# A layer's input projection by Strassen-Winograd products: when the saved partial products are read back

## The chip, the cores and the metric

One core of a Trainium2 chip runs the kernel; the seven other cores are idle. The metric is device time of one execution in microseconds. Three runs of the kernel before gave 1662.98, 1666.43 and 1667.63 us, so the median is 1666.43 us. The profile shows one further execution, which took 1667.98 us.

## The reference

One layer of a streaming encoder with 1024 tokens and width 2048, all in float32. One projection of the input gives ten blocks of columns; a sparse attention group (each query keeps its 256 best keys by a light indexer) and a Mamba-2 state-space group (causal convolution, chunked scan, gated RMS norm) work on them; both are gated, joined, projected back, added to the scaled input and normalised:

```python
u = jnp.einsum('bsd,de->bse', h, w_in[layer])
q, k, v, z_attn, q_idx, k_idx, w_idx, z_ssd, xbc, dt_raw = _split_cols(u, IN_WIDTHS)
o_attn = _dsa_attention(q, k, v, q_idx, k_idx, w_idx) * jax.nn.silu(z_attn)
o_ssd = _ssd_mixer(xbc, z_ssd, dt_raw, conv_w[layer], ...)
mixed = jnp.concatenate([o_attn, o_ssd.astype(o_attn.dtype)], axis=-1)
sub = jnp.einsum('bse,ed->bsd', mixed, w_out[layer])
h = _layer_norm(DEEPNORM_ALPHA * h + sub, ln_g[layer], ln_b[layer])
```

The change concerns the first line, the input projection.

## The kernel before, in words

**Number format.** Every float32 operand of the two projections is split into a high and a low part: ACT rounds the high part (`xh` of the input, `wh` of the weights), DVE subtracts it to get the low part (`xl`, `wl`). A product is three matmuls: `wh` with `xh`, `wh` with `xl`, `wl` with `xh`.

**Units.** The input projection is cut into 190 units, numbered 0 to 189 here in the order in which PE runs them (the list `pieces` of `units()`). A unit is a 128-column block of weights times half the input's depth: eight blocks of depth by three matmuls of 128x512, that is 24 matmuls into one PSUM bank (`pj`). Four banks have that name. The output projection follows as units 190 to 245. Between the matmuls of a unit the program places PE work of the other parts: indexer scores, attention, state-space scan.

**Seven products for eight.** Most weight blocks are handled in pairs by a Strassen-Winograd scheme (`product()`), seven units for what eight would do, in four phases. There are two groups of pairs: group 0 with 8 pairs, group 1 with 14. In a phase the pairs go in couples: first half-unit of both, then second half-unit of both. Phase 0's first unit is saved to DRAM as P1 (`t_save`, copied out of PSUM by ACT). Phase 1 adds P1 to its two units and saves the sums as U2 and U3 (`t_u`, on DVE). Phases 2 and 3 add U2 or U3 to what PE has computed (`t_comb`, on DVE) and hand the result on. In phases 0 to 2 the second unit of a pair accumulates on top of the first one's PSUM bank, so PE may not begin it before ACT or DVE has read the bank (the event `after`); that unit comes two units after the first.

**The loads concerned.** A saved partial product comes back by one 256 KB load from DRAM into a buffer of tag `u` (128x512 float32). There are 29 such buffers, used by nearly everything in the kernel. `pre_ld()` makes a task of it, and `t_ld()` asks for a free buffer with two more to spare (`u=1, keep=2`) and for the saved data to be there; then it puts the load on SP's queue. There are 88 of these loads. The DVE addition that uses one is placed after the last matmul of the unit.

**What sets the order.** Every engine runs its instructions in the order in which the program was written, and that order is written by a planner in the kernel (`Flow`): it keeps a list of tasks by priority, and at four points of each unit (`pump`) lets every task that is ready by its own cost table write its next instructions. `hooks` are calls at the start of a unit: requests for partial products, requests for the next set of inputs, and so on. The table of costs only decides the order; on the chip, each instruction waits for what it needs and blocks the later ones of its engine. Weights are loaded up to eight units ahead, and the split into `wh` and `wl` is written up to two units ahead where data and buffers allow (`w_split`, `need_w`).

In the profile every instruction has line L312, since one helper writes them all; groups are told apart by the names of tiles. `u<-pj,u` and `cv<-pj,u` on DVE are the additions of a partial product; `u<-u` on SP's queue is a load of U2 or U3 or a save of one (110 in all), `u<-p` a load of P1 (22), `p<-u` a save of P1.

Of the kernel before, what the change touches and what calls it, by code (L numbers as in the profile page):

```python
# [582 lines left out]
class Layer:  # L583
# [20 lines left out]
    def units(self):  # L604

        pieces, work = [], []
        self.hooks = {}
        self.sets = []
        self.mate = {}

        def put(p, listed=True):
            if listed:
                work.append((len(pieces), None))
            pieces.append(p)
            return len(pieces) - 1

        def plain(h, tile, u, n):
            kind, j = tile
            t = ORDER.index(tile)
            p = Piece("T", h, t, u, load=(("w", t, u),), n=n + u, open=u == 0, close=u == 1, key=(h, t),  # L620
                      s0=256 if (kind == "qi" and h == 0) else 0)
            if u == 1:
                p.done = lambda ps: self.fl.add(getattr(self, "t_" + kind)(h, j, ps), 0, f"{kind}{j}h{h}", self.fl.t + 100)
            put(p)

        for pairs in PLAN:
            if isinstance(pairs, tuple):
                h, tiles, end = pairs
                n = len(self.sets)
                self.sets += [("x", h, 0), ("x", h, 1)]  # L630
                for part in [tiles[:3]] + [[t] for t in tiles[3:-end]] + [tiles[-end:]]:
                    for u in range(2):
                        for tile in part:
                            plain(h, tile, u, n)
                continue
            gi = GROUPS.index(pairs)
            if self.sets[-2:] != [("x", 0, 0), ("x", 0, 1)]:
                self.sets += [("x", 0, 0), ("x", 0, 1)]
            base = len(self.sets) - 2
            self.sets += [("f", "M2"), ("f", "M3"), ("f", "S1"), ("f", "S4"), ("x", 1, 1)]  # L640
            couples = [list(range(c, min(c + 2, len(pairs)))) for c in range(0, len(pairs), 2)]
            if len(couples[-1]) == 1:
                couples[-2:] = [couples[-2] + couples[-1]]
            for ph in range(4):
                if (gi, ph) in ((0, 2), (1, 0)):
                    self.hooks.setdefault(len(pieces), []).append(lambda on=gi == 0 and ph == 2: setattr(self.fl, "resting", on))
                for couple in [int(k) if k.isdigit() else k for k in OPENING] if (gi, ph) == (0, 0) else couples:
                    if isinstance(couple, str):
                        tile = ("misc", 0) if couple == "m" else QI["abcdefgh".index(couple)]
                        for u in range(2):  # L650
                            plain(0, tile, u, base)
                        continue
                    couple = couples[couple] if isinstance(couple, int) else couple
                    for f in range(1 + (ph < 3)):
                        for c in couple:
                            i = put(self.product(gi, c, pairs[c], ph, f, base + 2 * ph + f))
                            if f:
                                self.mate[gi, c, ph] = i
                            if ph and (ph, f) != (1, 1):
                                self.hooks.setdefault(max(i - 1, 0), []).append(lambda gi=gi, c=c, ph=ph, f=f: self.pre_ld(gi, c, ph, f))  # L660
        end = {}
        for i, p in enumerate(pieces):
            end[p.n] = i
        for i in end.values():
            pieces[i].last = True
        freed = sorted(end, key=end.get)
        for n in range(2, len(self.sets)):
            at = end[freed[n - 2]] - 2
            self.hooks.setdefault(at, []).append(lambda n=n: self.request(n))
        self.n_t = len(pieces)  # L670
        self.hooks.setdefault(self.n_t - 6, []).append(lambda: self.forms(0))
        self.hooks.setdefault(12, []).append(self.form_tasks)
        for half in range(2):
            self.hooks.setdefault(12, []).append(lambda half=half: self.fl.add(self.t_wsum(half), 5, "wsum"))
        for n in range(7):
            for d in range(2):
                for j in range(4):
                    if n < 6 or 4 * d + j < 8 - SKEW:
                        work.append((len(pieces), (0, 1, 2, 3)))
                    name = PRODUCTS[n][1]  # L680
                    pieces.append(Piece("O", n, d, j, load=(("o", name, d, j),)))
        for sts in ((0,), (1,), (2,), (3,)):
            work += [(len(pieces) - SKEW + j, sts) for j in range(SKEW)]
        return pieces, work
# [1672 lines left out]
```

## Time and profile before

| What | Value |
|---|---|
| Median of three runs | 1666.43 us (1662.98 to 1667.63) |
| The profiled execution: time, and span of its instructions | 1667.98 us, 1666.1 us |
| PE busy, share of the span | 1620.1 us, 97% |
| DVE busy | 1321.7 us, 79% |
| ACT busy | 1002.0 us, 60% |
| POOL busy | 197.3 us, 12% |
| DMA packets | 414.48 MB, mean 249 GB/s |
| Mean granted TensorE clock | 0.992 |

A wait in brackets in the order of time is the idle time of the engine just before the instruction, with what ended it. In the table of waits each row gives who waited for whom, microseconds in total, how often, and the longest. The 1.9 us between the profiled execution's time and its span lie outside of the instructions. The second group of the input projection runs from about 570 to 1313 us, the output projection from there to 1654 us, and the last 11 us have no matmul.

### The profile page before, as it was taken

To read this page: it belongs to the slowest core of one execution; us is meant where nothing else is said; L and a number is where in the kernel's file an instruction comes from. 1 tells how busy PE (TensorE), PEld (TensorE's weight loads), DVE (VectorE), ACT (ScalarE), POOL (GpSimd) and SP (SyncE) were. 2 spreads that over 40 slices of the span, in tenths; PEclk is the share of its full clock that TensorE was granted. 3 is DMA by queue.
4 is the path that set the end of the run, shared out by engine and by line. 5 is a ranking of instruction groups with operands and counts; after the bars stand their busy time and mean duration, and the time that the engine had idled before them with its cause. 6 is when DMAs were issued, how large, how long until landed. Compare 5 with 4: busy or idle time off the path is not lost. (4 is left out here: it accounts for less than half of the span.)

```text
span 1666.1 us, 23979 instructions
## 1 busy us (share of the span) xinstructions
PE 1620.1 (97%) x7996; PEld 1340.9 (80%) x7996; DVE 1321.7 (79%) x2429; ACT 1002.0 (60%) x1770; POOL 197.3 (12%) x215
## 2 busy tenths in 40 slices
PE   9999999999998989999999999999999999999997
PEld 7787777888787768888888888888877888888885
DVE  5889998997778866788676669875787687659998
ACT  4555666779787788776344456776866555532330
POOL 0100010000000000122212202222010000100110
PEclk9999999999999999999999999999999999999999
DMA  8177574789768856687786584656988889668664
GB/s 309 52 280 258 189 262 168 268 303 334 290 230 324 294 196 234 235 304 277 260 288 218 180 286 161 210 171 210 334 284 307 316 300 325 215 232 274 220 202 152
DMA packets 192387, 414.48 MB, mean 249 GB/s; under 512 B 19720, under 2 KB 55688, under 8 KB 192264
## 3 DMA queue, kind: packets, MB, share of 16 engines
q1 hardware_dynamic: 191832, 412.56, 71.7%
q8 instruction: 63, 1.03, 0.2%
q14 instruction: 60, 0.49, 0.1%
q10 hardware_dynamic: 432, 0.39, 0.1%
HBM read 308.94 MB, written 103.94 MB: 248 GB/s over the span
## 5 line engine op out<-in xcount | busy, mean ns | idle before, releaser
L312 PE MATMUL pj<-xh,wh 128*128 128x512 f32 (+1 forms) x1496 | 585.7, 392 | 14.5 <-ACT u L312 6.0
L312 PE MATMUL pj<-xh,wl 128*128 128x512 f32 (+1 forms) x1496 | 573.6, 383 | 5.1 <-DVE wl L312 5.1
L312 PE MATMUL pj<-xl,wh 128*128 128x512 f32 (+1 forms) x1496 | 573.0, 383 | 0.0
L312 DVE TENSOR_TENSOR wl<-wr,wh 128x1024 fp32r<-128x1024 f32 (+2 forms) x236 | 282.4, 1201 | 172.4 <-ACT wh L312 170.4
L312 PEld LDWEIGHTS pj<-xh,wh 128*128 128x128 f32 x1496 | 283.8, 190 | 68.6 <-issue 7.5
L312 PEld LDWEIGHTS pj<-xh,wl 128*128 128x128 f32 x1496 | 283.5, 190 | 63.1 <-DVE wl L312 7.3
L312 PEld LDWEIGHTS pj<-xl,wh 128*128 128x128 f32 x1496 | 284.0, 190 | 49.1
L312 ACT ACTIVATE wh<-wr 128x1024 fp32r<-128x1024 f32 (+2 forms) x242 | 248.1, 1031 | 120.0 <-PE pj L312 82.8
L312 PE MATMUL a<-u,u 128*128 128x512 f32 (+3 forms) x736 | 172.8, 354 | 7.6 <-DVE s L312 4.4
L312 PEld LDWEIGHTS a<-u,u 128*128 128x128 f32 x736 | 120.7, 189 | 42.5 <-DVE s L312 18.6
L312 ACT ACTIVATE u<-a 128x512 fp32r<-128x512 f32 (+4 forms) x115 | 53.2, 479 | 153.3 <-DVE u L312 58.0
L312 ACT ACTIVATE u<-s,sm 128x640 bf16<-128x640 int16 (+7 forms) x132 | 129.7, 983 | 22.1 <-DVE sm L312 20.0
L312 DVE TENSOR_TENSOR u<-u,u 128x512 f32<-128x512 f32 (+6 forms) x204 | 128.6, 645 | 5.7 <-DMA u<-wo 1.3
L312 PE MATMUL pj<-wh,xh 128*128 128x512 f32 x310 | 125.2, 404 | 0.5 <-DVE u L312 0.5
L312 PE MATMUL pj<-wh,xl 128*128 128x512 f32 x310 | 121.0, 390 | 0.0
L312 PE MATMUL pj<-wl,xh 128*128 128x512 f32 x310 | 121.0, 390 | 0.0
L312 ACT ACTIVATE a<-a 128x512 f32<-128x512 f32 (+3 forms) x160 | 77.1, 505 | 68.3 <-PE a L312 65.5
L312 ACT ACTIVATE u<-u 128x512 f32<-128x512 f32 (+4 forms) x146 | 80.1, 558 | 52.4 <-DVE u L312 43.9
L312 DVE TENSOR_TENSOR u<-pj,u 128x512 f32<-128x512 f32 (+2 forms) x112 | 74.7, 668 | 45.7 <-PE pj L312 42.2
L312 DVE TENSOR_TENSOR wr<-wr,wr 128x1024 f32<-128x1024 f32 (+1 forms) x81 | 99.8, 1233 | 0.8 <-DMA wr<-wt 0.4
L312 POOL TENSOR_SCALAR s<-s,sm 128x640 f32<-128x640 f32 (+7 forms) x64 | 63.8, 1011 | 124.0 <-DVE sm L312 97.4
L312 DVE SCALAR_TENSOR_TENSOR u<-cv,cw,u 128x512 f32<-128x512 f32 x96 | 73.0, 766 | 6.7 <-ACT u L312 3.5
(259 smaller groups left out, 2200.3 us busy)
## 6 DMA issues: line engine op xcount, KB each, us to landing
wr<-wt SPq DMA_DIRECT2D x187, 512.0 KB
u<-u SPq DMA_DIRECT2D x110, 256.0 KB
wr<-t SPq DMA_DIRECT2D x44, 512.0 KB
u<-wo SPq DMA_DIRECT2D x64, 256.0 KB
ts<-u SPq DMA_DIRECT2D x64, 256.0 KB
wr<-ts SPq DMA_DIRECT2D x32, 512.0 KB
s<-xt SPq DMA_DIRECT2D x24, 512.0 KB
t<-wr SPq DMA_DIRECT2D x22, 512.0 KB
```

The source lines that it names most:

```text
L312: f(*args, **kw)
```

## The change

The request for a partial product is hooked at the start of the unit two before the one that it is added to, where it was one before. Buffers, priorities and costs stay.

```diff
@@ units() @@
                             if ph and (ph, f) != (1, 1):
-                                self.hooks.setdefault(max(i - 1, 0), []).append(lambda gi=gi, c=c, ph=ph, f=f: self.pre_ld(gi, c, ph, f))
+                                self.hooks.setdefault(max(i - 2, 0), []).append(lambda gi=gi, c=c, ph=ph, f=f: self.pre_ld(gi, c, ph, f))
```

Of the 88 loads, 85 stand earlier against PE's units, nearly all by one unit. Since the planner then finds other buffers free at each point, the order of everything after the first such load changes with it. Rows of the two orders follow; numbers at the end of a name tell buffers apart and differ between the programs.

SP's queue where the first loads stand, during units 50 to 53, before. `p1_0_0` and `p1_0_1` are P1 of pairs 0 and 1, `xf...` and `wt` are inputs and weights, `c0_0` takes a result:

```order
L312 DMA p1_0_7_3490<-u_629_3476 128x512
L312 DMA xr_632_3498<-xfM32_107 128x1024
L312 DMA s4_633_3506<-xfM33_108 128x1024
L312 DMA wr_638_3530<-wt 128x1024
L312 DMA wr_639_3531<-wt 128x1024
L312 DMA wr_640_3532<-wt 128x1024
L312 DMA u_646_3553<-p1_0_0_1661 128x512
L312 DMA c0_0_333<-u_635_3518 128x512
L312 DMA u_666_3626<-p1_0_1_1741 128x512
```

The same place with the change:

```order
L312 DMA p1_0_7_3490<-u_629_3476 128x512
L312 DMA u_632_3492<-p1_0_0_1661 128x512
L312 DMA xr_633_3500<-xfM32_107 128x1024
L312 DMA s4_634_3508<-xfM33_108 128x1024
L312 DMA wr_639_3532<-wt 128x1024
L312 DMA wr_640_3533<-wt 128x1024
L312 DMA wr_641_3534<-wt 128x1024
L312 DMA u_647_3555<-p1_0_1_1741 128x512
L312 DMA c0_0_333<-u_636_3520 128x512
```

The load of P1 of pair 0 has passed five loads of inputs and weights, and that of pair 1 one save.

DVE before unit 65 (phase 1, pair 7), before. `wl_740` is the low part of unit 65's weights, `pj_743` the bank of unit 64, so the addition `u_746<-pj_743` waits for unit 64's last matmul:

```order
L312 TENSOR_TENSOR u_718_4052<-pj_722_4085,u_718_4052 128x512
L312 TENSOR_SCALAR u_738_4242<-s4_107_743,sm_518_2843 128x640
L312 SCALAR_TENSOR_TENSOR s4_107_743<-u_738_4242,s4_107_743 128x640
L312 TENSOR_TENSOR wl_740_4247<-wr_725_4103,wh_739_4246 128x1024
L312 TENSOR_TENSOR wl_742_4251<-wr_710_3993,wh_741_4250 128x1024
L312 TENSOR_SCALAR u_745_4278<-s4_108_744,sm_518_2843 128x768
L312 TENSOR_TENSOR u_746_4286<-pj_743_4254,u_731_4189 128x512
```

With the change `wl_744` is the low part of unit 65's weights and `pj_739` the bank of unit 64:

```order
L312 TENSOR_TENSOR u_706_3985<-u_706_3985,u_728_4178 128x512
L312 TENSOR_TENSOR u_705_3983<-u_705_3983,u_706_3985 128x512
L312 TENSOR_TENSOR u_742_4279<-pj_739_4232,u_727_4142 128x512
L312 TENSOR_TENSOR wl_744_4282<-wr_725_4116,wh_743_4281 128x1024
L312 TENSOR_TENSOR wl_746_4286<-wr_711_4001,wh_745_4285 128x1024
L312 TENSOR_TENSOR wl_748_4290<-wr_723_4114,wh_747_4289 128x1024
```

The split of unit 65's weights stood a unit ahead of the addition for unit 64; now it stands right behind it.

SP's queue at the state-space scan of the second half's head group 0 (loads of `hst0`, `c1_0`, `arow1`), before; `p1_1_12` is added after unit 144:

```order
L312 DMA u_1766_9788<-v0_1_344 128x512
L312 DMA u_1768_9802<-hst0_279 128x256
L312 DMA u_1769_9804<-c1_0_337 128x2x256
L312 DMA u_1770_9805<-c1_0_337 128x2x256
L312 DMA s4_1771_9808<-arow1_284 128x512 x2
L312 DMA u3_1_10_9826<-u_1685_9370 128x512
L312 DMA u_1779_9828<-p1_1_12_7358 128x512
```

With the change; `u2_1_12` is added after unit 174:

```order
L312 DMA mx1_5_276<-u_2147_11700 128x512
L312 DMA u_2200_11986<-hst0_279 128x256
L312 DMA u_2201_11988<-c1_0_337 128x2x256
L312 DMA u_2202_11989<-c1_0_337 128x2x256
L312 DMA s4_2203_11992<-arow1_284 128x512 x2
L312 DMA u_2209_12006<-zs0_3_324 128x2x256
L312 DMA u_2213_12029<-o0_2_307 128x512
L312 DMA u_2214_12031<-u2_1_12_9844 128x512
```

This scan, whose loads wait for many free buffers, begins during unit 171 instead of unit 142.

## Prediction

> **What bounds the kernel now.** I read the page first, then the stretches, PE's waits, DVE's waits, and last the order of time at the longest of them.
>
> ```profile
> span 1666.1 us, 23979 instructions
> PE 1620.1 (97%) x7996; PEld 1340.9 (80%) x7996; DVE 1321.7 (79%) x2429; ACT 1002.0 (60%) x1770; POOL 197.3 (12%) x215
> ...
> 0.00:335.00 335.00, 322.79 (x1581) 262.15 (x1582) 282.61 (x476) 200.44 (x354) 21.05 (x31) 0.99 0.63 224
> 1310.00:1500.00 190.00, 189.84 (x1006) 158.31 (x1006) 131.74 (x234) 93.47 (x167) 13.80 (x14) 1.00 0.79 276
> ...
> L312 SPq DMA_DIRECT2D u<-p x22: 320/428/783, 335.7 to 991.5; - x22
> ```
>
> PE is the bound: it is busy for 97% of the span, and the change leaves it the same matmuls. Only its waits can change, and its clock behind them. The stretches (length, then busy PE, weight loads, DVE, ACT, POOL, clock, DMA share, GB/s) show 12.2 us without PE before 335 us and 0.2 us from 1310 to 1500. The first load concerned was issued at 335.7 us and moves up by one unit, so nothing much earlier changes. What is open to the change are PE's waits from 335 to 1310 us:
>
> ```profile
> PE pj L312 <- ACT u L312: 6.0, 2, 4.3
> PE pj L312 <- DVE u L312: 5.2, 2, 4.9
> PE pj L312 <- DVE wl L312: 2.5, 3, 1.4
> PE a L312 <- DVE u L312: 2.4, 3, 1.5
> PE pj L312 <- ACT wh L312: 1.9, 2, 1.6
> PE a L312 <- DVE sm L312: 1.1, 3, 0.5
> PE a L312 <- POOL sm L312: 0.6, 1, 0.6
> PE a L312 <- ACT u L312: 0.6, 1, 0.6
> PE a L312 <- POOL u L312: 0.5, 1, 0.5
> PE o L312 <- DVE u L312: 0.4, 1, 0.4
> ```
>
> They add up to 21.2 us, and none of them is a wait for a DMA: the loads can reach PE only through DVE. That sum is the most that a better order could give, apart from the clock; a worse order has no such bound.
>
> **The loads themselves.** DVE waits for a returned partial product three times in the whole run, 5.0 us together (its table of waits), the longest at 571.37 us:
>
> ```profile
> DVE u L312 <- DMA u<-u: 2.5, 2, 1.7
> DVE cv L312 <- DMA u<-u: 2.5, 1, 2.5
> ...
> 454.55 0.69 DVE L312 TENSOR_TENSOR u<-pj,u 128x512 f32<-128x512 f32 x1 [1.65 <-DMA u<-u]
> 455.30 0.55 PE L312 MATMUL a<-c,u 128*128 128x128 f32 x3 [0.30 <-DVE u L312]
> ...
> 560.69 0.48 SPq L312 DMA_DIRECT2D u<-u  x1
> 571.37 0.69 DVE L312 TENSOR_TENSOR cv<-pj,u 128x512 f32<-128x512 f32 x1 [2.49 <-DMA u<-u]
> 573.10 0.28 ACT L312 ACTIVATE u<-a 128x128 f32<-128x128 f32 x1 [5.59 <-DVE u L312]
> 585.10 0.57 ACT L312 ACTIVATE u<-pj 128x512 f32<-128x512 f32 x1
> 583.38 0.39 PE L312 MATMUL pj<-xl,wh 128*128 128x512 f32 x1
> 583.60 0.39 PE L312 MATMUL pj<-xh,wl 128*128 128x512 f32 x1
> 585.73 0.50 PE L312 MATMUL pj<-xh,wh 128*128 128x512 f32 x1 [1.74 <-ACT u L312]
> ```
>
> The load issued at 560.69 is awaited until 571.37, 10.7 us, where PE's matmuls follow each other by 0.23 us, so a unit of 24 takes 5.5 us and the lead of one unit, counted to the end of the unit, is 11 us. The loads arrive just in time, and in three places not quite. One more unit gives 16.4 us and takes these waits away. What is that worth on PE?
>
> - At 455.30 PE waited 0.30 us behind the late addition: gain 0.3.
> - At 571.37 the late addition held DVE for 2.49 us, ACT's next instruction came at 573.10 after 5.59 us of idleness, and ACT's copy of a bank, at 585.10, was what PE waited for at 585.73. If ACT starts 2.5 us earlier, the wait goes: gain 1.7.
> - The third, by the table 0.85 us (2.5 less 1.65), has no PE wait behind it: nothing.
>
> So the edit proper gives 2.0 us. If the queue of ACT is as late as before for another reason, it gives 0.3; more than 2.0 is not to be had, since no other wait leads back to such a load.
>
> **What moves with it.** The order of all engines changes from there on, and the waits that I can place by the two orders are these:
>
> ```profile
> 544.57 0.50 PE L312 MATMUL pj<-xh,wl 128*128 128x512 f32 x1 [1.42 <-DVE wl L312]
> ...
> 516.26 1.22 DVE L312 TENSOR_TENSOR wl<-wr,wh 128x1024 fp32r<-128x1024 f32 x1
> 517.40 1.23 DVE L312 TENSOR_TENSOR wr<-wr,wr 128x1024 f32<-128x1024 f32 x1
> 518.54 0.68 DVE L312 TENSOR_TENSOR u<-pj,u 128x512 f32<-128x512 f32 x1
> 519.37 0.77 PE L312 MATMUL pj<-xh,wh 128*128 128x512 f32 x1 [4.89 <-DVE u L312]
> ```
>
> - The low weights of three units (57, 68 and 87) are written one unit earlier than before. These are the three places at which PE waited for `wl`, 2.5 us in the table, the longest at 544.57. Gain 2.5.
> - At 519.37 PE waits 4.89 us for an addition that stands at the end of a DVE queue: eight `xl`, two sums of weights, one `wl`. Its load had long landed. In the new order one sum of weights has left the queue ahead of it; one such step is 1.14 us (516.26 to 517.40). Gain 1.1; the rest of this wait stays.
> - The longest wait for ACT, 4.3 us before unit 99, lies behind eight exponentials of the state-space scan. ACT's rows ahead of that copy are the same in both orders: nothing.
> - Unit 65 is the one place where the new order writes a unit's weights only when it begins. Its `wl` stands behind the addition that reads unit 64's bank. From unit 64's last start: 0.39 for the matmul, 0.6 for the addition (0.68 less the overlap of 0.09 seen between 516.26 and 517.40), 1.22 for `wl`, together 2.2 us. Two matmuls of unit 65 need no `wl`; the third would have started 0.7 us after that last start. New wait: 1.5 us. DVE's own lateness could double it; if ACT and DVE got to it early, it could not be less than this, since the addition needs the bank.
> - Unit 209, in the output projection: ACT rounds the input for it behind an exponential batch and a weight block in the new order, where before the batch came after.
>
> ```profile
> 614.28 1.28 ACT L312 ACTIVATE u<-s 64x512 f32<-64x512 f32 x2
> 615.58 2.44 ACT L312 ACTIVATE s<-s,ac 128x128 f32<-128x128 f32 x8
> ...
> L312 ACT ACTIVATE wh<-wr 128x1024 fp32r<-128x1024 f32 (+2 forms) x242 | 248.1, 1031 | 120.0 <-PE pj L312 82.8
> ```
>
>   These are 1.3, 2.4 and 1.0 us, 4.7 together, of which about 2.7 (half a unit) lie beside unit 208. Between nothing (ACT gets ahead) and 3 us; I take 1.5, nearer to the other waits of this kind.
> - The clock. After some waits PE is granted half speed for a while, and its matmuls follow by 0.43 us instead of 0.23. It happens behind the 4.89 us at 519.37 and behind a wait of 1.48 us, not behind the 1.42 us at 544.57 nor the 1.74 us at 585.73:
>
> ```profile
> 1279.40 0.61 PE L312 MATMUL a<-o,u 128*128 128x1 f32 x4 [1.48 <-DVE u L312]
> 1280.38 0.63 PE L312 MATMUL pj<-xl,wh 128*128 128x512 f32 x1
> 1280.81 0.63 PE L312 MATMUL pj<-xh,wl 128*128 128x512 f32 x1
> ...
> 516.00:520.00 4.00, 0.63 (x2) 0.56 (x3) 4.00 (x6) 0.50 (x1) 0.05 (x1) 0.84 0.99 383
> 520.00:524.00 4.00, 4.00 (x15) 3.20 (x14) 2.64 (x7) 2.32 (x4) 1.19 (x2) 0.73 1.00 385
> ```
>
>   One such stretch costs (0.16 + 0.27) x 4 = 1.7 us by the clock column of the two windows. Of the three waits of 1.4 to 1.7 us one brought it on, so each of the two new waits is charged a third: 1.1 us in all, between 0 and 3.4. The Trainium skill, in "TensorE: Matmul & The Clock Gate", section "What's actually happening", says that the half rate comes after at least one idle window of about 3.4 us. By that rule this charge would be nothing and the forecast 1.1 us lower; the row at 1279.40, half speed behind 1.48 us, disagrees, and the measurement decides.
> - The rest, 21.2 less 2.0 + 2.5 + 1.1 and less what stays of the two long waits (3.8 + 4.3), is 7.5 us of small waits, mostly behind attention and the scan. The new order deals them anew. I take the same sum again; nothing to twice as much are the bounds.
>
> **The sum.** Gains 2.0 + 2.5 + 1.1 = 5.6; costs 1.5 + 1.5 + 1.1 = 4.1; net 1.5 us less. The profiled execution took 1667.98 us, its span and 1.9 us around it, so the sum is 1666.5. It was 1.5 us above the median of the runs, 1666.43; against that the sum is 1664.9. The forecast lies between the two: **1665.5 us**, no change that can be told. A difference of 0.3%, 5 us, is about what measurements of this kernel can tell; the three runs alone spread over 4.7 us.
>
> **The rivals.**
>
> *Slower: buffers.* Each load holds one of 29 `u` buffers for one unit longer, and tasks that want many at once wait for them. The order shows it: the scan of head group 0's second half begins in unit 171 instead of 142. Its work falls on units 171 to 193 and delays what it displaces into the output projection, where PE hardly waits today (0.2 us of 190). Before 335 us, with DVE at 84% against 69% there (282.61 of 335, 131.74 of 190), PE was without work for 3.6%. That share over some 220 us from unit 171 on (it would begin near 1180 us) is 8 us; one stretch at half speed adds 1.7 us, and about as much of today's waits there falls away, so +8 on the sum of 1666: 1674. It decides if PE's waits after 1180 us pass 10 us. For it: DVE has little room there, and unit 65 shows that the order can put a split last. Against it: the total of DVE's and ACT's work is the same, and the scan has no one waiting for it until the output projection's later products. The skill's "Perfetto Trace Analysis", section "Identifying Performance Opportunities", says that a gap repeating on the engine that should be saturated can mean that there isn't buffer room for the next tile; no such repeated gap is in the trace of before.
>
> *Faster: the long wait goes.* If the queue ahead of the addition at 518.54 arrives earlier as a whole, since the loads no longer bunch with the requests for inputs, the other 3.8 us and the half speed behind them (1.7) go too, and of the small waits half may fall away (3.7). That is 9.2 us more than the forecast: 1656; with only the first two, 1660. For it: DVE's backlog there is of a few large items. Against it: the items that stay, eight `xl` and two weight blocks, are not loads of partial products.
>
> *The change doesn't do what it says.* Where no buffer is free, an earlier request only queues earlier. At a handful of the 88 loads that is so (three stand no earlier), not at the three late ones. Gain nothing, costs as above: 1666 to 1670.
>
> **How the numbers follow.** The forecast (gains and new waits cancel) 0.43, slower by buffers 0.27, faster 0.25, no effect of the loads 0.05. Within 0.3% are the forecast and most of the last: 0.46. Faster by over 0.3%, that is under 1661.4, 0.26; slower, over 1671.4, 0.28. The forecast's own range, from its terms' bounds (2.0 to 0.3 for the loads, 0 to 3 for unit 209, 0 to 3.4 for the clock, 7.5 up or down for the small waits taken half), is 1660 to 1671. The range of 8 in 10 reaches into both rivals: 1657 to 1675.
>
> **What would show it.** Right: DVE's waits for `u<-u` fall from 5.0 us to under 1; PE no longer waits 1.4 us for `wl` near 545, nor for ACT near 585; a new wait of 1.5 us or a little more for `wl` three matmuls into unit 65, near 413; the waits near 519 and 618 remain, the first about 3.8 us. Wrong: PE waiting for DVE or ACT by more than 10 us after 1180 us (the buffers); no wait over 2 us near 519 (the faster rival); PE's matmuls other than 7996, or time before 325 us that differs by more than 1 us (then something other than this order changed).

## The result, and the profile after

| | before | after |
|---|---|---|
| Median | 1667.03 us (1662.98 to 1669.01) | 1680.35 us (1677.25 to 1681.29) |
| Profiled execution, and its span | 1667.98 us, 1666.1 us | 1677.25 us, 1675.1 us |
| Mean granted TensorE clock | 0.992 | 0.988 |

The change made the kernel slower by 13.3 us: the ratio is 1.0086, with a 95% interval from 1.0068 to 1.0104. The predicted time was 1665.5 us, the range 1657 to 1675, so the forecast and its range both missed, on the slow side.

The work is the same. The page of after:

```profile
span 1675.1 us, 23976 instructions
PE 1622.1 (97%) x7996; PEld 1341.5 (80%) x7996; DVE 1322.5 (79%) x2433; ACT 1001.5 (60%) x1770; POOL 201.6 (12%) x216
```

PE has the same 7996 matmuls, and DVE and ACT are busy as long as before, to within 1 us. So the time went into PE's waits and its clock. PE's waits from 335 to 1310 us, the same stretch of which the prediction shows the table of before (who waits for whom, total, times, longest):

```profile
PE pj L312 <- DVE u L312: 6.5, 2, 6.2
PE pj L312 <- ACT u L312: 5.8, 3, 4.0
PE pj L312 <- DVE wl L312: 4.8, 2, 4.3
PE a L312 <- DVE u L312: 3.1, 5, 1.3
PE a L312 <- DVE sm L312: 2.5, 5, 0.8
PE o L312 <- DVE u L312: 2.3, 2, 1.3
PE a L312 <- ACT u L312: 0.9, 2, 0.6
```

They add up to 25.9 us, against 21.2 before. From 1310 us on the same table has two rows in before, 0.7 us:

```profile
PE pj L312 <- DVE u L312: 0.5, 2, 0.3
PE a L312 <- DVE u L312: 0.2, 1, 0.2
```

and two in after, 4.8 us:

```profile
PE pj L312 <- ACT xh L312: 2.6, 1, 2.6
PE pj L312 <- DVE u L312: 2.2, 2, 1.8
```

PE's order of time in after at the places of which the prediction spoke, and at one of which it did not (1367.24):

```profile
414.04 0.80 PE L312 MATMUL pj<-xh,wl 128*128 128x512 f32 x1 [4.30 <-DVE wl L312]
...
521.43 0.76 PE L312 MATMUL pj<-xh,wh 128*128 128x512 f32 x1 [6.16 <-DVE u L312]
...
584.62 0.50 PE L312 MATMUL pj<-xh,wh 128*128 128x512 f32 x1 [0.48 <-ACT u L312]
...
619.06 0.80 PE L312 MATMUL pj<-xh,wh 128*128 128x512 f32 x1 [4.03 <-ACT u L312]
...
1367.24 0.50 PE L312 MATMUL pj<-wh,xh 128*128 128x512 f32 x1 [1.84 <-DVE u L312]
...
1368.30 0.63 PE L312 MATMUL pj<-wl,xh 128*128 128x512 f32 x1
...
1453.55 0.78 PE L312 MATMUL pj<-wh,xh 128*128 128x512 f32 x1 [2.57 <-ACT xh L312]
```

The clock follows the waits. Stretches of half speed, the last one after the end of the matmuls left out, add up to 20.5 us in before and 30.7 us in after. Some of that time PE was waiting anyway, so the price is half of the time in which it had work. From 335 us on there are three such stretches in before and five in after; the sums of their windows (length, then PE's busy time) are these:

```profile
sum 13.65, PE 12.23 PEld 9.90 DVE 8.09 ACT 10.03 POOL 1.54; mean PE 4.08 PEld 3.30 DVE 2.70 ACT 3.34 POOL 0.51
sum 27.28, PE 20.84 PEld 16.06 DVE 23.64 ACT 14.45 POOL 2.10; mean PE 4.17 PEld 3.21 DVE 4.73 ACT 2.89 POOL 0.42
```

Half of 20.84 less 12.23 is 4.3 us. The largest new loss lies behind the wait at 414.04. The windows of after:

```profile
414.00:420.00 6.00, 5.96 (x15) 4.73 (x16) 5.33 (x9) 4.45 (x8) 0.00 (x0) 0.55 0.96 298
...
1310.00:1500.00 190.00, 185.31 (x980) 153.64 (x979) 132.79 (x239) 102.01 (x185) 15.31 (x16) 0.98 0.79 263
```

PE is busy from 414 to 420 us, but at a clock of 0.55: 15 matmuls, where full speed makes 26. In the output projection PE is busy for 185.31 of 190 us, where before had 189.84.

**The sum by the trace.** Waits 25.9 less 21.2 from 335 to 1310 us, 4.7; from 1310 us on 4.8 less 0.7, 4.1; half speed 4.3: together 13.1 us. The spans differ by 9.0 only. Ahead of unit 50 PE's order is the same in both programs, and there the profiled execution of before lost 3.6 us more than that of after (time from each matmul's start to the next, above what its form usually takes). The largest such place in before:

```profile
231.73 1.88 PE L312 MATMUL a<-u,u 128*128 128x512 f32 x4 [2.01 <-DVE s L312]
```

So 3.6 us there are chance of two executions: from 335 us on after is slower by 9.0 + 3.6, that is 12.6 us, near to the 13.1 of the sum and the 13.3 us of the medians. The prediction had named a difference of more than 1 us before 325 us as a sign that something else had changed; it came, with the same order on both sides, so that bound was too narrow for two executions.

By the same measure of lost time, after less before is: units 50 to 63 -1.2 us, 64 to 91 +5.4, 92 to 187 -1.0, 188 to 197 +0.9, 198 to 219 +8.4, the rest -0.4. Two places make the loss: the stretch from unit 65 to the wait at 521, and the output projection.

### The profile page after: what moved, and what is told of

The parts are those of the page before. It is cut to its first block, busy times and chain, and to the rows that moved or that the text cites. A ratio compares the mean times of both kernels' runs of the same rounds, so it can differ in the third digit from the quotient of the medians.

```text
span 1675.1 us, 23976 instructions
## 1 busy us (share of the span) xinstructions
PE 1622.1 (97%) x7996; PEld 1341.5 (80%) x7996; DVE 1322.5 (79%) x2433; ACT 1001.5 (60%) x1770; POOL 201.6 (12%) x216
## 5 line engine op out<-in xcount | busy, mean ns | idle before, releaser
L312 PE MATMUL pj<-xh,wh 128*128 128x512 f32 (+1 forms) x1496 | 585.0, 391 | 13.3 <-DVE u L312 6.2
L312 PE MATMUL a<-u,u 128*128 128x512 f32 (+3 forms) x720 | 169.3, 353 | 6.0 <-DVE s L312 1.9
L312 ACT ACTIVATE u<-s,sm 128x640 bf16<-128x640 int16 (+7 forms) x132 | 129.6, 982 | 14.9 <-DVE sm L312 12.9
L312 DVE TENSOR_TENSOR u<-u,u 128x512 f32<-128x512 f32 (+7 forms) x210 | 134.1, 649 | 4.2 <-issue 1.1
L312 PE MATMUL pj<-wh,xh 128*128 128x512 f32 x318 | 130.2, 409 | 4.9 <-ACT xh L312 2.6
L312 PE MATMUL pj<-wh,xl 128*128 128x512 f32 x318 | 125.6, 395 | 0.1
L312 PE MATMUL pj<-wl,xh 128*128 128x512 f32 x318 | 125.3, 394 | 0.0
L312 DVE TENSOR_TENSOR wr<-wr,wr 128x1024 f32<-128x1024 f32 x78 | 95.3, 1223 | 2.0 <-DMA wr<-wt 1.6
L312 PEld LDWEIGHTS pj<-wh,xh 128*128 128x128 f32 x318 | 60.4, 190 | 19.8 <-DVE u L312 4.3
```

The source lines that it names most:

```text
L312: f(*args, **kw)
```

## Experiments: the loads without the new order

The edit does two things: it asks earlier, and by that it deals the order of all engines anew. Three theories. *Loads:* an earlier request itself costs something (buffers, SP's queue). *Named waits:* the few new waits that the trace shows make the loss, and go with their causes. *Order as such:* the order before is a favourable one, and any order dealt anew is slower.

For the first I recorded the order in which the program of before writes its work, and wrote it again from that list, with loads moved and nothing else. In the first two such kernels each tile also took the number of its buffer from the list where that was free.

**All loads that the change moves**, on the order of before:

```diff
 PE, DVE, ACT, POOL: the order of before
 SP, for 85 of the 88 loads:
-  start of the unit before the addition's:  u<-p1 / u<-u2 / u<-u3
+  one unit earlier:                         u<-p1 / u<-u2 / u<-u3
```

> The order of PE, DVE, ACT and POOL is that of the kernel before, instruction by instruction; only in SP's queue 85 of the 88 loads of partial products stand one unit earlier, as the change asks (three find no free buffer there and stay). This is the edit without what the planner made of it. Theory 'the loads themselves did what was said, and the slower time comes from the order that was dealt anew': DVE's waits for returned partial products go from 5.0 us to under 1, PE's waits at 455.3 (0.3 us) and 585.7 (1.7 us) go, and the time is 0 to 3 us under the kernel before, 1664 to 1667. Rival 'the loads themselves cost, because each holds a buffer for one unit longer and crowds SP's queue': 1670 or more, with PE's or DVE's waits grown by over 3 us. Rival 'two units of lead bring nothing that can be seen': within 1 us of the kernel before, though the DVE waits are gone.

Measured: 1670.3 us against 1663.36; 1.0039 (1.0026 to 1.0052). From unit 50 up to unit 184 PE lost as much time as in before, within 0.4 us; then 6 us more in units 184 and 185. SP's queue there, in before:

```profile
1261.85 0.50 SPq L312 DMA_DIRECT2D u<-hst  x1
```

and in this kernel, with PE behind it:

```profile
1269.61 0.32 SPq L312 DMA_DIRECT2D u<-hst  x1
```

```profile
1274.67 0.33 PE L312 MATMUL a<-c,u 128*128 128x128 f32 x1 [1.52 <-DMA u<-c]
...
1283.38 1.01 PE L312 MATMUL a<-o,u 128*128 128x1 f32 x4 [3.88 <-DVE u L312]
```

The load of the scan's state was issued 7.8 us later, because by my list it took a buffer that another tile held until then. That is a flaw of the experiment, not of the change: the kernel could have taken another buffer. **The 71 loads of units up to 174**, so that none lies near that scan, with the same numbers of buffers:

> As the first kernel with the loads alone (order of PE, DVE, ACT and POOL instruction by instruction that of the kernel before), but only the 71 loads that stand before unit 175 are a unit earlier; the later ones, where a load of the scan's state in SP's queue was held for a buffer until 1269.6 us and not 1261.9, stay where they were. Theory 'the loads do what was said, and cost only where buffers are short': PE's excess stays 1 to 3 us under the kernel before all the way, 1 to 3 us faster than it: ratio 0.998 to 0.999; the 4.0 us wait at 1279 is 1.5 us again. Rival 'an earlier load costs by itself, by crowding SP's queue': ratio 1.002 or more, as with all the loads (1.0039).

Measured: 1672.35 us against 1664.49; 1.0041 (1.0026 to 1.0056). From unit 50 to 100 it gained 3.5 us on before; it lost 2 us and a stretch at half speed near 800 us, and 5.2 us near 1278, by the same flaw. It settles nothing on the loads; it shows what a wrong buffer costs. **The same 71 loads, each tile taking the buffer that was given back first**, which is the planner's own rule:

> The 71 loads before unit 175 a unit earlier, all other instructions in the order of the kernel before, as in the second kernel with loads alone; but every tile now takes the free buffer that was given back first, where that kernel gave the scan's state at unit 182 a buffer that another tile of the scan still held until 1270 us. Theory 'the loads cost only where a buffer is short': the waits of 5.2 us at 1278 and 2.2 us near 798 go, PE's excess stays 1 to 4 us under the kernel before to the end: ratio 0.998 to 0.9995. Rival 'a buffer held a unit longer is missed somewhere, whichever is given': ratio 1.002 to 1.004 again, with waits for released buffers at other places.

Measured: 1663.07 us against 1663.41; 0.9993 (0.9982 to 1.0005). No row of DVE's waits names `u<-u` any more. DVE's addition at the place where before waited 2.49 us (571.37):

```profile
567.34 0.69 DVE L312 TENSOR_TENSOR cv<-pj,u 128x512 f32<-128x512 f32 x1
```

PE's wait of 1.74 us at 585.73 is gone, the next one for ACT is there as before:

```profile
614.51 0.80 PE L312 MATMUL pj<-xh,wh 128*128 128x512 f32 x1 [3.90 <-ACT u L312]
```

So these 71 earlier loads in the old order are worth between 3.0 us gained and 0.8 lost. That holds the prediction's 2.0, and does not tell it from nothing. The 14 later loads stood as in before here. The first kernel moved them and the second did not, both with the flaw of the buffers, and their ratios, 1.0039 and 1.0041, don't differ. What this excludes is that earlier loads by themselves cost 13 us.

**The three late loads alone** were to say whether those suffice. By a slip of mine the kernel moved the loads of units 71, 78 and 91, where the third late one is that of unit 90:

```diff
 SP:
-  loads of units 71, 78, 91 in units 70, 77, 90
+  loads of units 71, 78, 91 in units 69, 76, 89
```

> Only the three loads on which DVE waits in the kernel before (those of units 71, 78 and 90) are issued a unit earlier; everything else stands in the order of the kernel before. It measures what the prediction called the loads themselves: 2.0 us (0.3 at 455 us, 1.7 at 586 us), and up to 2 us more if the wait for ACT near 614 us, 22 us later, shortens too. Ratio 0.997 to 0.9995 by the theory. Rival 'they bring nothing that shows': 1.000, with PE's wait of 1.7 us at 586 still there or given back within five units.

Measured: 1664.2 us against 1663.41; 1.0003 (0.9992 to 1.0014). The slip makes it a control, since the load of unit 90 is still issued at 558.55:

```profile
569.38 0.69 DVE L312 TENSOR_TENSOR cv<-pj,u 128x512 f32<-128x512 f32 x1 [2.60 <-PE pj L312]
```

```profile
583.74 0.61 PE L312 MATMUL pj<-xh,wh 128*128 128x512 f32 x1 [1.85 <-ACT u L312]
```

With that load late, the wait of PE stays; with it early (the kernel above), the wait goes. So the link from the load to ACT and PE that the prediction drew is there. The row at 569.38 names PE as the releaser, but PE's last matmul of that unit had started near 564.6. The row stands 10.8 us after the load's issue, as the one at 571.37 in before stood 10.7 us; the load is the likelier one.

## Experiments: the named waits repaired

These run the order of after, with single entries of its list moved. **Unit 65's weights split earlier:**

```diff
 DVE, order of after (the order of ACT stays):
+  12 instructions earlier, behind attention's first items in unit 64: low part (wl) of unit 65's weights
-  behind the addition of unit 64's bank: low part (wl) of unit 65's weights
```

> The changed kernel's order, with one step moved: the rounding of unit 65's weights (ACT's wh and DVE's wl) stands right behind the sum that makes these weights, in unit 64's first quarter, and no longer behind unit 64's bank addition. Theory 'three new waits with half speed behind them make the changed kernel slower': PE's wait of 4.5 us near 409 us and the 6.8 us at half speed (3.4 us lost) go: 1680.3 less 7.9, 1672 to 1674. Rival 'a wait removed there comes back at the next item in DVE's queue, since DVE itself is late': over 1677, with a wait of 3 us or more within the next two units.

Measured: 1676.2 us; 1.0080 of before (1.0067 to 1.0093), about 1 us better than after's 1.0086, which these intervals don't tell apart. The wait of 4.30 us is gone, and another stands two units later, with half speed behind it:

```profile
426.96 0.76 PE L312 MATMUL pj<-xh,wh 128*128 128x512 f32 x1 [2.66 <-ACT u L312]
```

**The waits of the output projection:**

```diff
 order of after:
-  loads of the residual (second and third) in unit 196; their copies in unit 197
+  the same loads in unit 194; their copies in unit 195
-  unit 209: exponentials of the scan, then the rounding of the input
+  unit 209: the rounding of the input, then the exponentials
```

> The changed kernel's order, with two places of the output projection repaired: the residual loads of output tiles 2 and 3 of the first half of the first product and the copies that free their banks stand where the kernel before has them (units 194 and 195 and not 196 and 197), and two roundings of unit 209's input on ACT stand ahead of the batch of exponentials and not behind it. Theory of three waits: PE's 2.0 us near 1365 and 2.7 us near 1451 go, with a stretch of half speed (1.7 us) behind each: 8 us, 1671 to 1674. Rival 'buffers: the scan that was moved holds the buffers, and the work is late there whatever stands first': over 1677, PE's waits after 1310 us stay over 3 us in sum.

Measured: 1677.87 us; 1.0081 (1.0067 to 1.0095). The waits at 1367 and 1453 are gone; waits of 1.09, 0.72, 1.31 and 1.34 us at 1357.77, 1373.47, 1376.45 and 1456.90 stand in their place. This kernel and the next have the flaw of the buffer numbers too: one load of the output projection was held back by some 3.4 us. **Both, and the sum of weights that after gives to POOL at 511.86 back on DVE:**

```diff
 both edits above, and
-  sum of weights 85: POOL
+  sum of weights 85: DVE
```

> The changed kernel's order with the repairs of both kernels above, and the sum of unit 85's weights given to DVE and not to POOL (near 512 us, where a DVE instruction of 0.7 us took 2.9 us beside POOL's sum). Theory of three waits: 7.9 and 8.1 us go, and 1 to 3 us of the 6.2 us wait near 515: 1680.3 less 17 to 19, 1661 to 1664, not slower than the kernel before. Rival 'any order dealt anew is some 13 us worse than the tuned one, in many small waits': 1671 or more, PE's waits under 1 us grown in sum by 5 us against the kernel before.

Measured: 1675.67 us; 1.0069 (1.0055 to 1.0083). The wait near 521 is still there:

```profile
520.90 0.77 PE L312 MATMUL pj<-xh,wh 128*128 128x512 f32 x1 [6.38 <-DVE u L312]
```

Repairs aimed at three places, expected to give 17 to 19 us, gave 2.8 us by the two ratios (1.0086 and 1.0069), some 8 us at most by their intervals; a load held for 3.4 us is too little to hide the rest. One of the three waits was not removed by its repair, and where the others went, new ones came. The theory of the named waits falls: they were where the loss showed, not what made it. The rival, that a new order loses in many small waits, doesn't hold in its form either: PE's waits under 1 us from 335 us on add up to 7.1 us here, against 6.4 in before, and those over 1 us to 22.3, against 15.4.

## Experiments: other orders, with one unit of lead and with two

For the third theory the planner dealt new orders from unit 50 on by a constant of its own, first with the loads where before has them. `MARGIN` (lines 362 and 441, 300 ns) is how long by the cost table a PE task's inputs must have been done before it is written; `SLACK` (lines 361 and 455, 2650 ns) is how far an engine's queue may reach ahead when a task is written.

```diff
-        self.hooks = {}
+        self.hooks = {50: [lambda: setattr(self.fl, "MARGIN", 250.0)]}
```

The others set `SLACK` to 2600, 2700 and 2550 in the same way.

> The kernel before, lead of one unit, with the planner's margin for a ready input 250 and not 300 ns from unit 50 on: the order is dealt anew from about the same place as by the change, with no load requested earlier. Theory 'what made the changed kernel slower is that the order was dealt anew and not what was asked for': slower too, ratio 1.003 to 1.01. Rival 'the longer hold of the buffers made it slower': the scatter of a new order is small, ratio 0.998 to 1.003.

> A second order dealt anew without an earlier load: the kernel before with the planner's slack (how far an engine's queue may run ahead of PE) 2600 and not 2650 ns from unit 50 on. Theory 'a new order as such': ratio 1.003 to 1.01, by other waits at other places than in the changed kernel. Rival 'buffers held longer': ratio 0.998 to 1.003.

> Lead of one unit, a third order dealt anew from unit 50 (slack 2700 ns and not 2650). Theory 'a new order as such': 5 to 15 us slower than the kernel before, as with the first two (7 and 14 us). Rival 'buffers held longer': ratio 0.998 to 1.003.

> A fifth pair, lead of one unit: slack 2550 ns from unit 50. So far the three new orders with a lead of one took 1.0042 to 1.0083 times the kernel before. 'A new order as such' expects the same of this one, 1.003 to 1.010.

Then the same four with the change's two units of lead:

> Lead of two units, margin 250 ns from unit 50: the partner of the order that with a lead of one took 1.0083 times the kernel before. Theory 'a new order as such': between 1.003 and 1.013, no worse on average than with a lead of one. Rival 'buffers held longer': the partner and 8 us or more on top, over 1.013.

> Lead of two units, slack 2600 ns from unit 50: the partner of the order that with a lead of one took 1.0043 times the kernel before. Theory 'a new order as such': between 1.003 and 1.013. Rival 'buffers held longer': over 1.009.

> Lead of two units, slack 2700 ns from unit 50: the partner of the first kernel of this call. Theory 'a new order as such': between 1.003 and 1.013, as its partner within 8 us either way. Rival 'buffers held longer': 8 us or more slower than its partner.

> Its partner with a lead of two units. In the four pairs so far the one with two units was slower by 0.0025 to 0.0086 of the kernel before. 'The longer hold of buffers adds to it' expects this partner 4 to 14 us slower too; 'a new order as such' expects either sign.

| Planner | one unit of lead | two units | difference |
|---|---|---|---|
| as it was | before, 1 | after, 1.0086 (1.0068 to 1.0104) | 0.0086 |
| MARGIN 250 | 1679.21 us, 1.0083 (1.0068 to 1.0097) | 1688.33 us, 1.0145 (1.0125 to 1.0165) | 0.0062 |
| SLACK 2600 | 1671.5 us, 1.0043 (1.0031 to 1.0056) | 1675.6 us, 1.0068 (1.0041 to 1.0095) | 0.0025 |
| SLACK 2700 | 1671.53 us, 1.0042 (1.0029 to 1.0056) | 1680.68 us, 1.0101 (1.0082 to 1.0120) | 0.0059 |
| SLACK 2550 | 1680.11 us, 1.0096 (1.0079 to 1.0113) | 1699.23 us, 1.0212 (1.0192 to 1.0232) | 0.0116 |

Two things are read from it. Down the first column: orders dealt anew without any earlier load are all slower, by 0.42 to 0.96%, 7 to 16 us, on average 0.66%. Across: two units are slower than one in all five rows, on average by 0.70% (0.28 to 1.12% as a 95% interval of five differences), some 11.6 us. The first row is no clean pair, since the order of before is better than all that the other settings gave; without it the four differences average 0.66% (0.06 to 1.25%), 10.9 us. So these new orders cost, and the longer lead costs on top of it, by an amount that these pairs hardly fix; in a single kernel such as after the two can't be told apart. Nor do four kernels show whether a new order as such is worse, or a constant other than the one that the kernel came with. Of what was expected, the pairs with `MARGIN` 250 and `SLACK` 2700 came out as for buffers held longer (over 1.013, and 9 us over the partner), `SLACK` 2600 as for a new order alone; the difference at `SLACK` 2550, 19 us, was above the 4 to 14 expected.

Where the longer lead costs: by the lost time of the profiles it adds some 8 us on average behind unit 171 and some 2 us in units 64 to 170. But the five pairs scatter widely: behind unit 171 four lose 8 to 22 us, and the one with `SLACK` 2600 gains 10 there and loses 14 before. One wait of the kernel with `MARGIN` 250 and two units, with what stands ahead of it on ACT and DVE:

```profile
1211.77 1.28 ACT L312 ACTIVATE u<-s 64x512 f32<-64x512 f32 x2
1213.08 2.45 ACT L312 ACTIVATE s<-s,ac 128x128 f32<-128x128 f32 x8
1215.43 1.13 ACT L312 ACTIVATE xh<-xr 128x512 fp32r<-128x512 f32 x2
1216.07 1.29 DVE L312 TENSOR_TENSOR xl<-xr,xh 128x512 fp32r<-128x512 f32 x2 [5.48 <-ACT xh L312]
1224.10 0.77 PE L312 MATMUL pj<-xh,wh 128*128 128x512 f32 x1 [9.51 <-DVE u L312]
```

PE waits for DVE, and DVE stood idle for 5.48 us until ACT, which had no idle time from 1202.60 us on, came to the rounding behind the scan's exponentials. No load and no buffer stands in this chain on the chip. Whether buffers are why the planner put the scan there, the trace can't show.

**Two units in group 0 alone, and three units everywhere**, as doses of the same edit:

```diff
-max(i - 2, 0)
+max(i - 1 - (gi == 0), 0)
```

> Two units of lead for the pairs of group 0 alone, one for group 1. Up to unit 118 the order is the changed kernel's: the waits near 409 (4.5 us) and 515 us (6.2 us) must be there. From there on it is a third order. Theory 'a new order as such': the loss of some 10 us between units 196 and 216 needn't be there, but waits elsewhere are: ratio 1.003 to 1.010. Rival 'buffers held longer by group 1's loads make the output projection wait': without them the loss after unit 196 goes, ratio 1.000 to 1.004.

Measured: 1684.17 us; 1.0118 (1.0105 to 1.0131), above both ranges expected.

```diff
-max(i - 2, 0)
+max(i - 3, 0)
```

> Three units of lead for all loads, the order dealt by the planner. Theory 'a new order as such, whatever the lead': 5 to 20 us slower than the kernel before, with no relation to the lead (two units: 1.0086). Rival 'buffers held longer': more lead holds more buffers, so clearly slower than with two units, ratio over 1.015.

Measured: 1687.63 us; 1.0142 (1.0120 to 1.0163). Three units are slower than after, but lie within the spread of the orders with two units in the table (1.0068 to 1.0212), so they don't show a cost that grows with the lead. And the lead in group 0 alone moves fewer loads and is slower than after: the size of the edit alone does not set the size of the loss.

## Experiment: a version that beats both

The two longest waits of before, near 519 and 618, stand behind queues of DVE and ACT. On the order of before:

```diff
 SP:  the 32 loads of group 0 one unit earlier
 DVE, behind unit 81's last matmul:
+  addition of unit 81's bank
   sum of weights; four low parts of the input (xl);
   low part of a weight block (wl); sum of weights
-  addition of unit 81's bank
 ACT, behind unit 97's last matmul:
+  copy of unit 97's bank
   two copies u<-s and eight exponentials of the scan
-  copy of unit 97's bank
```

> The order of the kernel before with the 32 loads of group 0 a unit earlier and two moves in the engines' order: the addition that reads unit 81's bank ahead of four of DVE's roundings and one sum of weights (PE's wait of 4.9 us at 514 us), and ACT's copy of unit 97's bank ahead of the eight exponentials of the scan (PE's wait of 4.3 us at 614 us). Theory 'PE's waits are made by the order of the queues and each is worth its length and its stretch at half speed, where the item moved has slack': loads 2 to 4, the first 4.9 and 1.7, the second 4.3 and 1.7 to 3.4: 14 to 18 us faster, ratio 0.989 to 0.992. Rival 'what is moved back makes PE wait a unit later', as in the kernels with repairs of the changed order: ratio 0.995 to 1.000.

Measured: 1660.17 us against 1663.41; 0.9977 (0.9968 to 0.9987). It is faster than before by 3.8 us, and so than after, where 14 to 18 were expected; the rival of that expectation, 0.995 to 1.000, holds. Two rows of its PE, and one of ACT ahead of the first:

```profile
531.22 0.82 ACT L312 ACTIVATE u<-cv,cw 128x512 f32<-128x512 f32 x1 [4.91 <-DVE cv L312]
...
536.80 0.56 PE L312 MATMUL pj<-xh,wh 128*128 128x512 f32 x1 [3.75 <-ACT wh L312]
...
627.41 0.50 PE L312 MATMUL pj<-xh,wh 128*128 128x512 f32 x1 [1.43 <-ACT u L312]
```

The wait at 519 is gone, and in units 82 and 83 PE lost 6.4 us less than in before; in units 84 to 87 it lost 7.2 us more. The second move kept some 4 us: 7.9 us lost in units 98 and 99 became 0.5, and 3.5 came back in units 100 to 111. That is one execution, and the kernel with three loads, where nothing is moved there, lost only 3.5 us in these two units, so the size is rough. The windows say why the first gain did not stay. Before, from 510 us:

```profile
510.00:520.00 10.00, 5.11 (x22) 3.94 (x21) 10.00 (x15) 6.50 (x13) 0.05 (x1) 0.94 0.95 350
520.00:530.00 10.00, 10.00 (x41) 8.19 (x40) 8.50 (x15) 8.29 (x16) 1.70 (x3) 0.89 0.72 276
530.00:540.00 10.00, 10.00 (x46) 8.29 (x45) 9.83 (x22) 5.65 (x9) 0.37 (x2) 1.00 0.84 292
```

and this kernel:

```profile
510.00:520.00 10.00, 10.00 (x46) 8.29 (x45) 9.93 (x16) 7.39 (x13) 2.45 (x2) 1.00 0.99 360
520.00:530.00 10.00, 9.78 (x44) 7.77 (x43) 9.89 (x14) 6.07 (x12) 0.52 (x1) 1.00 0.76 261
530.00:540.00 10.00, 4.40 (x17) 2.87 (x16) 9.75 (x21) 8.68 (x14) 1.97 (x4) 0.86 0.86 292
```

DVE, the third busy time of a row, has nearly no idle time to give: 1.5 us in the middle window of before, 0.4 us in all three of this kernel. PE's 5 us without work have only moved from the first window to the third, where ACT, which had itself waited 4.91 us for DVE (531.22), makes PE wait. DVE is the bound of that stretch, and a new order of its work does not shorten it. What does start late is the stretch itself: in before DVE's row just ahead of it is

```profile
509.17 1.23 DVE L312 TENSOR_TENSOR wl<-wr,wh 128x1024 fp32r<-128x1024 f32 x1 [4.08 <-ACT wh L312]
```

and this kernel has the same 4.08 us at 505.76. An earlier `wh` on ACT, to let DVE use them, is an experiment that was not run. Behind 618 ACT had room, and there a part of the gain stayed.

## Why the prediction was wrong

**The step that failed** is the last one of "What moves with it": "The new order deals them anew. I take the same sum again." It took a new order as neutral, with as much chance to be better as worse, and priced beside it only the places that two orders showed. Four new orders without any earlier load were 7 to 16 us slower. The order of before is better than its neighbours; why it is, the runs don't show. With two units of lead the four clean pairs add 10.9 us on average to it, and why the lead adds to it stays open too.

Term by term:

- **PE is the bound, no wait of PE for these loads**: right. After has none either.
- **The loads, 2.0**: right in mechanism, and the size is not told from nothing. DVE's 5.0 us of waits for `u<-u` are gone, the 1.74 us at 585.73 became 0.48. In the order of before the gain of 71 of them lies between 3.0 and -0.8 us.
- **Low weights of three units, 2.5**: the wait at 544.57 is gone, as said.
- **519, 1.1 gained**: wrong in sign, 4.89 became 6.16. The sum of weights did leave DVE's queue, but to POOL, where it ran beside DVE's `xl` and held one up (below). With it back on DVE the wait is 6.38: the backlog of DVE made the wait, not this one item.
- **618, nothing**: right, 4.31 became 4.03.
- **Unit 65, 1.5**: the place was right, the third matmul at 414.04; the size was 4.30. "DVE's own lateness could double it" was the bound named and passed over. DVE's order in after shows the lateness:

```profile
407.28 0.55 DVE L312 TENSOR_SCALAR u<-s,sm 128x640 bf16<-128x640 int16 x1
407.87 0.83 DVE L312 SCALAR_TENSOR_TENSOR s<-u,s 128x640 f32<-128x640 bf16 x1
...
410.84 1.41 DVE L312 TENSOR_TENSOR u<-u,u 128x512 f32<-128x512 f32 x2
412.17 0.68 DVE L312 TENSOR_TENSOR u<-pj,u 128x512 f32<-128x512 f32 x1
412.77 3.48 DVE L312 TENSOR_TENSOR wl<-wr,wh 128x1024 fp32r<-128x1024 f32 x3
```

  Attention's items, from 407.28 to 412.17, stand ahead of the addition that frees the bank; the `wl` comes behind both. I had counted from the bank, not from the queue.
- **Unit 209, 1.5**: 2.57, inside its bounds of 0 to 3.
- **The output projection otherwise, nothing**: 1.84 us at 1367.24 were missing in the sum.
- **The clock, 1.1**: 4.3 by the trace, above its bound of 3.4. It was charged to two waits of 1.5 us; behind the 4.30 us alone some 2.7 us were lost, behind 1.84 and 2.57 one stretch each. The price of 1.7 us for a stretch was read from windows in which PE also waited: behind the wait at 519.37 PE had work for 2.8 of 3.4 us, so that one cost 1.4.
- **Small waits, 7.5 again**: 25.9 less the four named (6.16, 4.03, 4.30, 0.48) is 10.9, so 3.4 more, inside the bounds.

So the terms were short by 2.4 at 519, 2.8 at unit 65, 1.1 at unit 209, 1.8 at 1367, 3.2 of clock and 3.4 of small waits, 14.7 together, nearly the 14.9 us by which the median missed the forecast. All six err to the same side. The small waits that the quoted sentence speaks of are thus about a quarter of the miss; the rest are places where the new order was priced too low one by one.

**The rivals.** Slower by buffers, 1674 us with a chance of 0.27, came nearest. Its mark, PE waits of more than 10 us after 1180 us, was not reached: 7.6 us, 3.2 before. What speaks for it is that the longer lead costs in all five pairs, in four of them mostly after unit 171, where it put its price. Against it, the one long wait there that was followed (1224.10) goes back to ACT's queue. By the two orders the loads hold 2.6 of the 29 `u` buffers on average in units 50 to 187, where they held 2.0, and 9.8 are free at the start of a unit where 10.8 were. That buffers are the cause is argued, not shown: a thirtieth doesn't fit into the core's memory, and no kernel with fewer was run. Faster, since the long wait goes, was wrong: the wait stayed, and where an experiment made it go, another came 17 us later.

## What to carry to other kernels

Where a program's order is written by a planner, an edit of one request is an edit of the whole order: price it by dealing the old kernel's order anew some four times by another constant, and take that mean as the base for the edit, not the tuned order's own time. Before a named wait is counted as a gain, look at the engine behind it in the windows around: where it had next to no idle time for the next 20 us, as DVE here, the wait moved and did not go. A wait behind a queue is counted from the engine's queue, with everything in it, not from the last event that it needs.

## What the hardware showed that I had not expected

The sum of weights on POOL held up a subtraction for a low part (`xl`) on DVE. POOL's and DVE's order of time in after, and the durations of that form by the view of one tile (shortest, median, longest in ns):

```profile
511.86 2.46 POOL L312 TENSOR_TENSOR wr<-wr,wr 128x1024 f32<-128x1024 f32 x1 [122.02 <-DVE xl L312]
```

```profile
510.76 4.71 DVE L312 TENSOR_TENSOR xl<-xr,xh 128x512 fp32r<-128x512 f32 x4
```

```profile
L312 DVE TENSOR_TENSOR xl<-xr,xh x53: 677/685/2903, 101.7 to 1201.8; 128x512 fp32r<-128x512 f32 x53
```

The four took 4.71 us, where the same four took 2.49 us in before (from 510.31); the one begun at 511.96, 0.1 us after POOL's sum, took 2.90, to about 0.5 us after POOL's end. The Trainium skill, "SBUF — State Buffer", section "🔬 SBUF: two separate sides", says that DVE with two inputs from SBUF and GpSimd share a pair of ports as an exclusive lock, and that the loser waits for the whole instruction; this row agrees.

PE went to half speed 1.1 us behind a wait of 1.84 us (1367.24 and 1368.30 above), and behind one of 2.57 us. The Trainium skill's rule of an idle window of about 3.4 us ("TensorE: Matmul & The Clock Gate", section "What's actually happening") does not give these; the waits that bring it on here are shorter. Their length alone does not decide: half speed followed 1.48 us at 1279.40 in before, and not 1.74 us at 585.73.
